# Stick-breaking columns in another order: earlier chains, wider stage spacing, and one pair's T1 built by DMA

## The chip, the cores and the metric

The kernel runs on one core of one Trainium2 chip. The metric is the device time of one execution in microseconds (us). Runs of the kernel before took 2211.62, 2213.59 and 2213.69 us, a median of 2213.59 us.

The engines are named as in the profile: PE is TensorE (PEld its weight loads), DVE is VectorE, ACT is ScalarE, POOL is GpSimd, SP is SyncE.

## The reference, cut to what matters

One layer of an encoder over 256 tokens of width 2048, all in float32: a SwiGLU feed-forward network (FFN), a mixer, a second FFN and an output gate, with layer norms between them. The mixer projects the normalised activations by one wide matrix `w_in` and feeds two attention branches:

```python
proj = x @ w_in
mq, mk, mv, mo, mi, mf, sq, sk, sv, ga, gb = _split_cols(proj)
y_m  = ...  # mLSTM, 4 heads of 256, from mq, mk, mv, gates mi and mf; times sigmoid(mo)
y_sb = _stick_breaking(_heads(sq, 8), _heads(sk, 8), _heads(sv, 8))   # 8 heads of 128
merged = sigmoid(ga) * (y_m @ w_up_m) + sigmoid(gb) * (y_sb @ w_up_sb)
return merged @ w_out
```

Stick-breaking attention, for each head and strictly causal (s < t):

```python
z = q @ k.T * dh ** -0.5
log_one_minus = where(strict, log_sigmoid(-z), 0)
cum = cumsum(log_one_minus); rem = cum[..., -1:] - cum
att = where(strict, exp(log_sigmoid(z) + rem), 0)
out = att @ v
```

## The kernel before, in words

**Matmuls.** Every weight matrix is cut into tiles of 256 rows by up to 512 columns (a *raw*, 512 KB), loaded by SP (`loads`, L1115). ACT casts a raw to a high part (L1142) and DVE subtracts to get the low part (L1146); the two are a *split*. A *unit* is one weight tile for one half of the tokens: six matmuls (L1191 to L1193) into one PSUM bank. A *group* is one block of up to 512 output columns: eight weight tiles for the 2048 rows, two units each, two banks.

**The order of work** is written out by hand as the list `program`. It is walked unit by unit; each unit adds 1.2966 to a planner's clock `sched.now`. Side work is a generator that yields delays (`DELAY`) and is resumed by `sched.run` after the unit at which it is due, so it enters each engine's queue at that point and the engines take their queues in order. Splits are made up to six tiles ahead and a limited number of raws is held (`HELD`: seven and six in the mode "wide", five and six in "mix").

**Pairs.** `seven` computes a pair of column blocks for both halves of the tokens with seven block products in place of eight (a Strassen scheme). Products 1 and 2 come first; then, in each of four quarters of the rows, products 5, 7, 6, 4 and 3, whose five accumulators stay open over all quarters. The weight combinations T1 = B11 + B12 and so on are made in place on the raws: by DVE (`plus`, L345), or, with `loaded`, T1 (and T3 of the last quarter) by an accumulating POOL DMA onto a loaded raw (L1119). The FFN uses `loaded`; the mixer's pairs, made by `both7`, do not. Products 5, 7, 6 and 3 use sums of the activations' quarters: `forms_later` (L309) adds high and low parts, and `form_turn` (L292 to L302) makes the combinations.

**The mixer's order** (L918 to L999): q and k columns of the mLSTM, with the gate columns and stick columns 0 and 1 in the second group (`gates_done`); v; o; then stick columns in groups of four heads, in plain order: 2 to 5, 6 to 9, 10 to 13, 14 to 17 (columns 0 to 7 are q heads, 8 to 15 k heads, 16 to 23 v heads). Then `weave` interleaves a main list (start of the sticks, stick columns 18 to 21 and 22 and 23, the gate branches of block 0, and three rounds of `ups`) with pairs 1, 2 and 3: three pair units after every four main units.

**Stick columns.** `sb_columns` evacuates a group's accumulator by ACT: v heads straight to their place (L684), q and k heads to a temporary (L688), which `sb_turn` transposes on PE 4.6 later (L694) and copies on DVE (L700), two heads a copy.

**Sticks.** `sticks` (L936) starts two chains: heads 0, 2, 4, 6, and 12.0 later heads 1, 3, 5, 7. A stick (L877) waits for its q, k and v, then: scores on PE (L882); ACT's scale, absolute value, exponential and logarithm, all at L225; DVE's maximum and sum (L891) and causal mask (L814); PE's running sum by a triangular matrix (L895, L896); DVE's subtraction (L897); ACT's exponential; DVE's mask (L814); PE's product with v (L906); and the evacuation by ACT (L269) and DVE (L270). Between the steps lie the delays sa, s0, s1, s2, s3, s4. `in_sequence` starts the next stick of a chain with no delay. Each PE result takes one of eight PSUM banks, which the groups and pairs use too. The sticks' results are read by the second half of `ups(0)`.

**mLSTM heads** (L816) run as two chains of two; DVE's product at L832 is followed, m1 later, by PE's L842.

Of the kernel before, what the change touches and what calls it, by code (L numbers as in the profile page):

```python
# [44 lines left out]
DELAY = {  # L45
    "alpha": 24.0, "away": 5.0, "sig": 1.5, "form": 18.0, "ln_turn": 3.6, "ln_step": 2.1, "gb": 14.0, "h": 8.0, "silu": 6.0, "late": 9.0, "rest": 1.2, "mt": 3.2,
    "sbt": 4.6, "g0": 3.0, "g1": 4.0, "g2": 12.0, "cv0": 1.0, "cv1": 3.5, "cv2": 1.3,
    "m0": 3.0, "m1": 0.6, "m2": 0.6, "m3": 4.6, "m4": 4.6, "sa": 1.4, "s0": 6.0, "s1": 6.0, "s2": 3.0, "s3": 4.0, "s4": 4.0,
}


# [113 lines left out]
def flat(pairs):  # L165
    return [u for p in pairs for u in p]
# [7 lines left out]
def kernel(  # L174
# [33 lines left out]
    def big(shape=(P, 1024)):  # L208
        return page_pool.tile(list(shape), F32, name="big", tag="page")
# [102 lines left out]


    def rows_of(w, r, col0, cols):
        return Raw(w[r:r + 2 * P, col0:col0 + cols].rearrange("(k p) c -> p k c", p=P), cols)

    def plain(raw):
        return Weight(raw, [raw], [raw])
# [11 lines left out]
    def seven(wa, ca, wb, cb, rows, cols, act, done, loaded):  # L330

        n = rows // (4 * P)
        accs = {m: {} for m in range(1, 8)}

        def unit(m, i, tile, src, half, sub):  # L340
            return Unit(tile, half, accs[m], src, i, sub, i == 0, i == n - 1, lambda ps, t, m=m: done(m, ps))

        def plus(out, a, b):
            def make():
                nc.vector.tensor_tensor(out=out.tile[:, :, :cols], in0=a.tile[:, :, :cols], in1=b.tile[:, :, :cols],  # L345
                                        op=ALU.add)
            return make

        units = []
        for m, sub in ((1, 0), (2, 2)):  # L350
            for i in range(n):
                units.append(unit(m, i, plain(rows_of(wa, (4 * i + sub) * P, ca, cols)), act, 0, sub))
        for i in range(n):
            b11, b12, b22, b21 = (rows_of(w, (4 * i + sub) * P, c, cols)
                                  for w, c, sub in ((wa, ca, 0), (wb, cb, 0), (wb, cb, 2), (wa, ca, 2)))
            if loaded:
                t1 = Raw(b12.src, cols, b11.src)
                first = Weight(t1, [t1], [])
            else:
                t1 = b11  # L360
                first = Weight(t1, [b11, b12], [], plus(b11, b11, b12))
            if loaded and i == n - 1:
                third = Weight(t3 := Raw(b12.src, cols, b22.src), [t3, b22], [t3])
            else:
                third = Weight(b12, [b12, b22] if loaded else [b22], [b12], plus(b12, b12, b22))
            units += [
                unit(5, i, first, act.forms, 0, 0),
                unit(7, i, third, act.forms, 1, 0),
                unit(6, i, Weight(t1, [], [], plus(t1, t1, b22), first), act.forms, 0, 2),
                unit(4, i, Weight(b21, [b21], [t1, b21], plus(b21, t1, b21)), act, 1, 2),  # L370
                unit(3, i, Weight(b22, [], [b22]), act.forms, 1, 2),
            ]
        return units

    def both7(w, ca, cb, act, dest, ready):

        r, held = {}, {}

        def put(k, t, a, b, op):
            nc.vector.tensor_tensor(out=r[k, t], in0=a, in1=b, op=op)  # L380

        def rest():
            u = r[0, 1]
            put(0, 1, held[7], u, ALU.add)
            z = r[1, 1] = dest(1, 1)
            nc.vector.scalar_tensor_tensor(out=z, in0=u, scalar=-1.0, in1=held[5],
                                           op0=ALU.mult, op1=ALU.subtract)
            ready(1, 1)
            return
            yield  # L390

        def done(m, ps):
            held[m] = ps
            if m == 1:
                r[0, 1] = dest(0, 1)
                nc.scalar.copy(r[0, 1], ps)
            elif m == 2:
                r[0, 0] = dest(0, 0)
                put(0, 0, ps, r[0, 1], ALU.add)
                ready(0, 0)  # L400
            elif m == 6:
                r[1, 0] = dest(1, 0)
                put(0, 1, ps, r[0, 1], ALU.add)
                put(1, 0, held[5], r[0, 1], ALU.add)
                sched.spawn(rest(), DELAY["rest"])
            elif m == 4:
                sched.until(lambda: (1, 1) in r)
                put(0, 1, ps, r[0, 1], ALU.add)
                ready(0, 1)
            elif m == 3:  # L410
                put(1, 0, ps, r[1, 0], ALU.subtract)
                ready(1, 0)

        return seven(w, ca, w, cb, D, COL, act, done, False)

    program = []

# [251 lines left out]

    sq0 = 2 * DM * HM + 2 * DM * HM + 2 * HM  # L670

    def sb_columns(ps, t, first, count):

        for which in range(3):
            lo, hi = max(first, 8 * which), min(first + count, 8 * which + 8)
            if lo >= hi:
                continue
            name = ("sq", "sk", "sv")[which]
            src = ps[:, (lo - first) * DS:(hi - first) * DS]
            if which == 2:  # L680
                if (name, t) not in st:
                    st[name, t] = big()
                cs = slice((lo - 16) * DS, (hi - 16) * DS)
                nc.scalar.copy(st[name, t][:, cs], src)  # L684
                flags.update((name, t, h - 16) for h in range(lo, hi))
            else:
                stage = temp()
                nc.scalar.copy(stage[:, :(hi - lo) * DS], src)  # L688
                sched.spawn(sb_turn(name, t, stage, lo - 8 * which, hi - lo), DELAY["sbt"])

    def sb_turn(name, t, stage, h0, n):
        ps = misc([P, 4, P])
        for k in range(n):
            nc.tensor.transpose(ps[:, k], stage[:, k * P:(k + 1) * P], ident[:])  # L694
        a = h0
        while a < h0 + n:
            b = min(h0 + n, (a // 4 + 1) * 4)
            if (name, "T", a // 4) not in st:
                st[name, "T", a // 4] = big().rearrange("q (h s) -> q h s", s=S)
            nc.vector.tensor_copy(out=st[name, "T", a // 4][:, a % 4:a % 4 + b - a, t * P:(t + 1) * P],  # L700
                                  in_=ps[:, a - h0:b - h0])
            a = b
        drop()
        flags.update((name, t, h) for h in range(h0, h0 + n))
        return
        yield

# [3 lines left out]
    def gates_done(ps, t):  # L711
        stage_g[t] = small.tile([P, 2 * HM], F32, name="gst", tag="gst", bufs=2)
        nc.scalar.copy(stage_g[t][:], ps[:, 0:2 * HM])
        sb_columns(ps[:, 2 * HM:], t, 0, 2)
        if t == TT - 1:
            sched.spawn(gates(), DELAY["g0"])

# [196 lines left out]
    def in_sequence(gens):  # L914
        for g in gens:
            yield from g
# [8 lines left out]
        program.extend(flat(group(w_in, range(0, D, 2 * P), 2048 + g * COL, COL, x1T, v_done(g))))  # L925
    for g in range(2):
        program.extend(flat(group(w_in, range(0, D, 2 * P), 3072 + g * COL, COL, x1T, mo_done(g))))
    def sb(first, n):
        return flat(group(w_in, range(0, D, 2 * P), sq0 + first * DS, n * DS, x1T,
                          lambda ps, t: sb_columns(ps, t, first, n)))  # L930

    program.extend(sb(2, 4) + sb(6, 4))
    program.append(lambda: [sched.spawn(forms_later(x1T, c), 14.0 + 14.0 * c) for c in range(4)])
    program.extend(sb(10, 4))

    def sticks():  # L936
        for a in (0, 1):
            sched.spawn(in_sequence([stick(a), stick(a + 2), stick(a + 4), stick(a + 6)]), 12.0 * a)


    mergedT = ActT(act_tile)
# [49 lines left out]
        return lambda k, t: sched.spawn(sigmoid(k, t), DELAY["sig"])  # L991

    def pair(g):
        return both7(w_in, ga0 + g * COL, ga0 + D + g * COL, x1T, gate_dest(g), gate_ready(g))

    program.extend(sb(14, 4))
    main = [sticks] + sb(18, 4) + sb(22, 2) + branch(0, 0) + branch(0, 1) + ups(0) + ups(1) + ups(2)
    mode("wide")
    program.extend(weave(main, pair(1) + pair(2) + pair(3)))  # L999
    mode("mix")  # L1000
# [108 lines left out]
    def loads(most=len(raws)):  # L1109
        while pos["load"] < most and pos["raw"] < (4 if pos["at"] < 6 else limits(pos["split"])[0]):  # L1110
            j = pos["load"]
            r = raws[j]
            r.tile = page_pool.tile([P, 2, COL], F32, name="raw", tag="page")
            for ks in pieces(j):
                nc.sync.dma_start(out=r.tile[:, ks, :r.cols], in_=r.src[:, ks])  # L1115
                if j == 0 and ks.start == 0:
                    load_x(0, 1)
            if r.plus is not None:
                nc.gpsimd.dma_start(out=r.tile[:, :, :r.cols], in_=r.plus, accum_op=ALU.add)  # L1119
            pos["load"] += 1  # L1120
            pos["raw"] += 1

# [106 lines left out]
```

## Time and profile before

| | |
|---|---|
| runs of the kernel before | 2211.62, 2213.59, 2213.69 us |
| the profiled execution | 2210.92 us |
| its span, first to last instruction | 2209.2 us |
| PE busy | 2186.7 us, 99% |
| DVE, ACT, POOL busy | 1873.8, 1294.3, 100.1 us |
| granted TensorE clock, mean | 0.999 |

The profile is of one execution. The page lists each engine's busy time; windows give it for a stretch; the waits say which instruction ended an engine's idle time; the timeline lists instructions with their start in us from the span's start. A row of a timeline ends with the idle time before it and what ended it, in brackets. In the waits the three numbers are the total in us, how often, and the longest. The mixer lies between about 660 and 1340 us.

### The profile page before, as it was taken

The numbers are of one execution on the slowest core, as the hardware profiler recorded it, in microseconds if no ns is written. First come the engines' busy times: TensorE is split into PE (matmuls) and PEld (weight loads), VectorE is DVE, ScalarE is ACT, GpSimd is POOL, SyncE is SP. The second block draws the span as 40 slices with busy tenths as digits, with TensorE's granted clock in tenths as the row PEclk, the third lists the DMA queues.
The fourth block names the chain that finished last, engine by engine and source line by source line (L and its number), as shares of the span: only waits on it lengthen the run. The fifth ranks groups of instructions, "written<-read, shape, count | busy, mean of one in ns | idle before, by whom it ended". The sixth has DMA issues, their size and how long they took to land. (4 is left out here: it accounts for less than half of the span.)

```text
span 2209.2 us, 28143 instructions
## 1 busy us (share of the span) xinstructions
PE 2186.7 (99%) x9990; PEld 1805.3 (82%) x9990; DVE 1873.8 (85%) x2089; ACT 1294.3 (59%) x1566; POOL 100.1 (5%) x88
## 2 busy tenths in 40 slices
PE   9999999999999999999899999999999999999999
PEld 7888888878888888788778888888888887888888
DVE  6999999998987874668879986699999999989774
ACT  7556655565655565545686554655565565656372
POOL 0100010000010000000000000000010001000000
PEclk9999999999999999999999999999999999999999
DMA  9899999999993675565768886589999999999553
GB/s 334 252 307 298 284 283 313 303 303 270 319 326 106 219 242 158 165 189 157 215 185 249 271 282 212 183 238 294 308 265 306 324 290 294 286 304 338 202 162 105
DMA packets 292365, 560.12 MB, mean 254 GB/s; under 512 B 17624, under 2 KB 26752, under 8 KB 292224
## 3 DMA queue, kind: packets, MB, share of 16 engines
q1 hardware_dynamic: 270464, 516.38, 70.0%
q0 software_dynamic: 21760, 41.95, 11.1%
q8 instruction: 78, 1.28, 0.2%
q14 instruction: 63, 0.52, 0.1%
HBM read 554.06 MB, written 4.19 MB: 253 GB/s over the span
## 5 line engine op out<-in xcount | busy, mean ns | idle before, releaser
L1146 DVE TENSOR_TENSOR split<-raw,split 128x1024 fp32r<-128x1024 f32 (+2 forms) x1049 | 1221.9, 1202 | 165.8 <-ACT split L1142 157.2
L1142 ACT CAST split<-raw 128x1024 fp32r<-128x1024 f32 (+2 forms) x1049 | 1043.2, 1036 | 503.6 <-DVE raw L345 184.8
L1191 PE MATMUL mm<-split,actT 128*128 128x512 f32 (+2 forms) x3128 | 1220.1, 390 | 6.4 <-DVE actT L270 3.1
L1192 PE MATMUL mm<-split,actT 128*128 128x512 f32 (+2 forms) x3128 | 1206.5, 386 | 1.7 <-DVE split L1146 1.5
L1193 PE MATMUL mm<-split,actT 128*128 128x512 f32 (+2 forms) x3128 | 1206.7, 386 | 0.6 <-DVE actT L282 0.6
L1191 PEld LDWEIGHTS mm<-split,actT 128*128 128x128 f32 x3128 | 588.7, 188 | 123.5 <-issue 3.8
L1192 PEld LDWEIGHTS mm<-split,actT 128*128 128x128 f32 x3128 | 588.8, 188 | 120.4 <-DVE split L1146 7.6
L1193 PEld LDWEIGHTS mm<-split,actT 128*128 128x128 f32 x3128 | 588.1, 188 | 121.0 <-DVE actT L282 1.4
L345 DVE TENSOR_TENSOR raw<-raw 128x1024 f32<-128x1024 f32 x224 | 273.3, 1220 | 2.3
L1119 POOL DMA_DIRECT2D raw<-in_ffn_w_dram x80 | 95.5, 1193 | 1879.4 <-DVE temp L543 812.3
L277 ACT CAST actT<-ms 128x512 fp32r<-128x512 f32 x60 | 35.0, 584 | 86.8 <-PE ms L275 85.8
L552 DVE TENSOR_TENSOR temp<-mm,temp 128x512 f32<-128x512 f32 x112 | 76.9, 686 | 5.6 <-PE mm L1193 3.8
L605 DVE SCALAR_TENSOR_TENSOR big<-mm,big 128x512 f32<-128x512 f32 x96 | 65.4, 685 | 16.3 <-PE mm L1193 16.1
L282 DVE TENSOR_TENSOR actT<-ms,actT 128x512 fp32r<-128x512 f32 x60 | 40.8, 684 | 22.9 <-ACT actT L277 11.7
L221 ACT ACT_TABLE_LOAD x35 | 44.9, 1283 | 0.6
L270 DVE TENSOR_TENSOR actT<-temp,actT 128x512 fp32r<-128x512 f32 x40 | 26.5, 688 | 17.3 <-ACT actT L269 17.2
L225 ACT ACTIVATE temp<-mm 128x512 f32<-128x512 f32 (+1 forms) x22 | 12.3, 560 | 44.1 <-PE mm L1193 44.1
L269 ACT CAST actT<-temp 128x512 fp32r<-128x512 f32 x40 | 24.2, 621 | 17.0 <-DVE temp L293 15.2
L225 ACT ACTIVATE temp<-temp 128x512 f32<-128x512 f32 (+1 forms) x48 | 28.5, 594 | 2.5 <-DVE temp L552 1.6
L780 DVE SCALAR_TENSOR_TENSOR temp<-ms,cw,temp 128x253 f32<-128x253 f32 (+2 forms) x48 | 23.1, 481 | 7.3 <-ACT temp L225 6.2
L225 ACT ACTIVATE rstd<-mv,eps 128x1 f32<-128x1 f32 x6 | 1.8, 295 | 45.9 <-DVE mv L462 45.9
L1012 DVE SCALAR_TENSOR_TENSOR big<-big,mm 128x512 f32<-128x512 f32 x8 | 5.5, 686 | 26.9 <-PE mm L1193 26.9
(126 smaller groups left out, 563.3 us busy)
## 6 DMA issues: line engine op xcount, KB each, us to landing
raw<-in_ffn_w_dram SPq DMA_DIRECT2D x655, 512.0 KB, 6.4
raw<-in_w_in_dram SPq DMA_DIRECT2D x192, 512.0 KB, 4.3
raw<-in_ffn_w_dram POOLq DMA_DIRECT2D x80, 512.0 KB, 9.1
raw<-in_w_out_dram SPq DMA_DIRECT2D x32, 512.0 KB, 5.1
raw<-in_w_ple_gate_dram SPq DMA_DIRECT2D x24, 512.0 KB, 5.7
raw<-in_w_up_m_dram SPq DMA_DIRECT2D x16, 512.0 KB, 5.4
raw<-in_w_up_sb_dram SPq DMA_DIRECT2D x16, 512.0 KB, 5.7
raw<-in_w_ple_gate_dram SPq DMA_DIRECT2D x16, 256.0 KB, 4.7
```

Of the source, the lines that this page charges most:

```text
L221: nc.scalar.preload_act_table_set(table[0])
L225: nc.scalar.activation(out, in_, func, **kw)
L282: nc.vector.tensor_tensor(out=dst[:, 1], in0=ps[:], in1=dst[:, 0], op=ALU.subtract)
L345: nc.vector.tensor_tensor(out=out.tile[:, :, :cols], in0=a.tile[:, :, :cols], in1=b.tile[:, :, :cols], op=ALU.add)
L552: nc.vector.tensor_tensor(out=out, in0=a, in1=b, op=op)
L605: nc.vector.scalar_tensor_tensor(out=xs, in0=ps, scalar=0.5, in1=xs, op0=ALU.mult, op1=ALU.add)
L1119: nc.gpsimd.dma_start(out=r.tile[:, :, :r.cols], in_=r.plus, accum_op=ALU.add)
L1142: nc.scalar.copy(hi[:, ks], r[:, ks])
L1146: nc.vector.tensor_tensor(out=lo[:, ks], in0=r[:, ks], in1=hi[:, ks], op=ALU.subtract)
L1191: nc.tensor.matmul(ps, hi, w[0][:, k, :u.cols], start=first, stop=False)
L1192: nc.tensor.matmul(ps, hi, w[1][:, k, :u.cols], start=False, stop=False)
L1193: nc.tensor.matmul(ps, lo, w[0][:, k, :u.cols], start=False, stop=last)
```

## The change

- **Order of the columns.** After the mLSTM's o columns come v heads 0 to 3, then a group of k heads 0, 1 and q heads 2, 3. Then the sticks start, ahead of the next groups (k 2, 3 and q 4, 5; v 4 to 7). The weave's main list begins with k 4, 5 and q 6, 7, then k 6, 7. The number and width of the groups are as before. A group of four q and k heads has two column ranges, so each of its raws is loaded by two DMAs of 256 columns.
- **Turns.** The copies after the transposes go from DVE to ACT, two heads a copy.
- **Sums of quarters.** `forms_later` starts after the first stick group, at 6, 24, 42 and 60, where it started after the second, at 14, 28, 42 and 56.
- **Stages.** m0, m1, m2 from 3.0, 0.6, 0.6 to 4.0, 2.0, 1.4; s0, s1, s3, s4 from 6.0, 6.0, 4.0, 4.0 to 7.0, 7.6, 5.0, 6.0; the second chain starts 14.0 after the first, not 12.0.
- **T1 of pair 1.** `both7` passes on `loaded`, true for pair 1 alone.

```diff
-    "m0": 3.0, "m1": 0.6, "m2": 0.6, "m3": 4.6, "m4": 4.6, "sa": 1.4, "s0": 6.0, "s1": 6.0, "s2": 3.0, "s3": 4.0, "s4": 4.0,
+    "m0": 4.0, "m1": 2.0, "m2": 1.4, "m3": 4.6, "m4": 4.6, "sa": 1.4, "s0": 7.0, "s1": 7.6, "s2": 3.0, "s3": 5.0, "s4": 6.0,
...
     def rows_of(w, r, col0, cols):
-        return Raw(w[r:r + 2 * P, col0:col0 + cols].rearrange("(k p) c -> p k c", p=P), cols)
+        ranges = col0 if isinstance(col0, list) else [(col0, cols)]
+        return Raw([w[r:r + 2 * P, c:c + n].rearrange("(k p) c -> p k c", p=P) for c, n in ranges], cols)
...
-        return seven(w, ca, w, cb, D, COL, act, done, False)
+        return seven(w, ca, w, cb, D, COL, act, done, loaded)
...
+    def sb_turn(t, stage, heads):
         ps = misc([P, 4, P])
-        for k in range(n):
+        for k in range(len(heads)):
             nc.tensor.transpose(ps[:, k], stage[:, k * P:(k + 1) * P], ident[:])
...
-            nc.vector.tensor_copy(out=st[name, "T", a // 4][:, a % 4:a % 4 + b - a, t * P:(t + 1) * P],
-                                  in_=ps[:, a - h0:b - h0])
...
+            nc.scalar.copy(st[name, "T", h // 4][:, h % 4:h % 4 + 2, t * P:(t + 1) * P], ps[:, k:k + 2])
...
-    program.extend(sb(2, 4) + sb(6, 4))
-    program.append(lambda: [sched.spawn(forms_later(x1T, c), 14.0 + 14.0 * c) for c in range(4)])
-    program.extend(sb(10, 4))
+    program.extend(sb(16, 17, 18, 19))
+    program.append(lambda: [sched.spawn(forms_later(x1T, c), 6.0 + 18.0 * c) for c in range(4)])
+    program.extend(sb(8, 9, 2, 3))
...
-            sched.spawn(in_sequence([stick(a), stick(a + 2), stick(a + 4), stick(a + 6)]), 12.0 * a)
+            sched.spawn(in_sequence([stick(a), stick(a + 2), stick(a + 4), stick(a + 6)]), 14.0 * a)
...
-        return both7(w_in, ga0 + g * COL, ga0 + D + g * COL, x1T, gate_dest(g), gate_ready(g))
+        return both7(w_in, ga0 + g * COL, ga0 + D + g * COL, x1T, gate_dest(g), gate_ready(g), g == 1)
...
-    program.extend(sb(14, 4))
-    main = [sticks] + sb(18, 4) + sb(22, 2) + branch(0, 0) + branch(0, 1) + ups(0) + ups(1) + ups(2)
+    program.append(sticks)
+    program.extend(sb(10, 11, 4, 5) + sb(20, 21, 22, 23))
+    main = sb(12, 13, 6, 7) + sb(14, 15) + branch(0, 0) + branch(0, 1) + ups(0) + ups(1) + ups(2)
...
-                nc.sync.dma_start(out=r.tile[:, ks, :r.cols], in_=r.src[:, ks])
+                at = 0
+                for src in r.src:
+                    n = src.shape[-1]
+                    nc.sync.dma_start(out=r.tile[:, ks, at:at + n], in_=src[:, ks])
+                    at += n
```

More of the change, by code (lines that the diff above doesn't have):

```diff
@@ L373, in seven, with both7 @@
         return units
-    def both7(w, ca, cb, act, dest, ready):
+    def both7(w, ca, cb, act, dest, ready, loaded):
         r, held = {}, {}
@@ L670 @@
     sq0 = 2 * DM * HM + 2 * DM * HM + 2 * HM
[L672 to L689, printed above, removed]
@@ L691, in sb_turn, with sb_columns @@
-    def sb_turn(name, t, stage, h0, n):
+    def sb_columns(ps, t, heads):
+        n = len(heads) * DS
+        if heads[0] >= 16:
+            if ("sv", t) not in st:
+                st["sv", t] = big()
+            c0 = (heads[0] - 16) * DS
+            nc.scalar.copy(st["sv", t][:, c0:c0 + n], ps[:, :n])
+            flags.update(("sv", t, h - 16) for h in heads)
+        else:
+            stage = temp()
+            nc.scalar.copy(stage[:, :n], ps[:, :n])
+            sched.spawn(sb_turn(t, stage, heads), DELAY["sbt"])
@@ L692, in sb_turn @@
+    def sb_turn(t, stage, heads):
         ps = misc([P, 4, P])
-        for k in range(n):
+        for k in range(len(heads)):
             nc.tensor.transpose(ps[:, k], stage[:, k * P:(k + 1) * P], ident[:])
[L695 to L700, printed above, removed]
-                                  in_=ps[:, a - h0:b - h0])
-            a = b
+        for k in range(0, len(heads), 2):
+            name, h = ("sq", "sk")[heads[k] // 8], heads[k] % 8
+            if (name, "T", h // 4) not in st:
+                st[name, "T", h // 4] = big().rearrange("q (h s) -> q h s", s=S)
+            nc.scalar.copy(st[name, "T", h // 4][:, h % 4:h % 4 + 2, t * P:(t + 1) * P], ps[:, k:k + 2])
+            flags.update([(name, t, h), (name, t, h + 1)])
@@ L703, in sb_turn @@
         drop()
-        flags.update((name, t, h) for h in range(h0, h0 + n))
         return
@@ L713, in gates_done @@
         nc.scalar.copy(stage_g[t][:], ps[:, 0:2 * HM])
-        sb_columns(ps[:, 2 * HM:], t, 0, 2)
+        sb_columns(ps[:, 2 * HM:], t, (0, 1))
         if t == TT - 1:
@@ L927, with sb @@
         program.extend(flat(group(w_in, range(0, D, 2 * P), 3072 + g * COL, COL, x1T, mo_done(g))))
-    def sb(first, n):
-        return flat(group(w_in, range(0, D, 2 * P), sq0 + first * DS, n * DS, x1T,
-                          lambda ps, t: sb_columns(ps, t, first, n)))
-    program.extend(sb(2, 4) + sb(6, 4))
-    program.append(lambda: [sched.spawn(forms_later(x1T, c), 14.0 + 14.0 * c) for c in range(4)])
-    program.extend(sb(10, 4))
+    def sb(*heads):
+        if heads[0] >= 16:
+            col0 = sq0 + heads[0] * DS
+        else:
+            col0 = [(sq0 + h * DS, 2 * DS) for h in heads[::2]]
+        return flat(group(w_in, range(0, D, 2 * P), col0, len(heads) * DS, x1T,
+                          lambda ps, t: sb_columns(ps, t, heads)))
+    program.extend(sb(16, 17, 18, 19))
+    program.append(lambda: [sched.spawn(forms_later(x1T, c), 6.0 + 18.0 * c) for c in range(4)])
+    program.extend(sb(8, 9, 2, 3))
     def sticks():
         for a in (0, 1):
-            sched.spawn(in_sequence([stick(a), stick(a + 2), stick(a + 4), stick(a + 6)]), 12.0 * a)
+            sched.spawn(in_sequence([stick(a), stick(a + 2), stick(a + 4), stick(a + 6)]), 14.0 * a)
     mergedT = ActT(act_tile)
@@ L1118, in loads @@
             if r.plus is not None:
-                nc.gpsimd.dma_start(out=r.tile[:, :, :r.cols], in_=r.plus, accum_op=ALU.add)
+                nc.gpsimd.dma_start(out=r.tile[:, :, :r.cols], in_=r.plus[0], accum_op=ALU.add)
             pos["load"] += 1
```

## The prediction

> **What bounds the kernel now.** The page comes first: its span and the busy shares.
>
> ```profile
> span 2209.2 us, 28143 instructions
> PE 2186.7 (99%) x9990; PEld 1805.3 (82%) x9990; DVE 1873.8 (85%) x2089; ACT 1294.3 (59%) x1566; POOL 100.1 (5%) x88
> ```
>
> TensorE (PE) is idle for only 22.5 us (2209.2 - 2186.7). The change removes no matmul, so it can win little more than PE's stops in the mixer. The table of 20 us windows over 880 to 1200 us shows where these lie; the columns are PE, PEld, DVE, ACT and POOL busy, the granted clock, the DMA share and GB/s.
>
> ```profile
> 880.00:900.00 20.00, 19.11 (x88) 15.30 (x87) 8.64 (x16) 9.75 (x15) 0.00 (x0) 1.00 0.54 157
> ...
> 920.00:940.00 20.00, 18.23 (x83) 14.96 (x83) 12.36 (x24) 11.18 (x16) 0.00 (x0) 1.00 0.58 172
> ...
> 980.00:1000.00 20.00, 20.00 (x94) 16.55 (x93) 14.14 (x21) 11.17 (x14) 0.00 (x0) 1.00 0.59 184
> ...
> 1020.00:1040.00 20.00, 20.00 (x91) 16.35 (x90) 19.69 (x27) 14.36 (x20) 0.00 (x0) 1.00 0.53 146
> 1040.00:1060.00 20.00, 16.96 (x84) 13.77 (x83) 18.36 (x25) 14.02 (x23) 0.00 (x0) 1.00 0.59 169
> 1060.00:1080.00 20.00, 19.97 (x110) 17.83 (x111) 17.70 (x21) 12.61 (x17) 0.00 (x0) 0.91 0.71 215
> 1080.00:1100.00 20.00, 17.31 (x87) 14.41 (x86) 17.40 (x21) 12.24 (x18) 0.00 (x0) 1.00 0.79 247
> ...
> 1140.00:1160.00 20.00, 17.18 (x74) 13.12 (x73) 16.36 (x19) 14.97 (x21) 0.00 (x0) 1.00 0.61 175
> ...
> sum 320.00, PE 307.72 PEld 252.42 DVE 241.33 ACT 196.35 POOL 0.00; mean PE 19.23 PEld 15.78 DVE 15.08 ACT 12.27 POOL 0.00
> ```
>
> Idle PE: 320 - 307.72 = **12.28 us**. Of it 2.66 lie in 880 to 940 (0.89 + 1.77, the mLSTM heads), 5.76 in 1040 to 1100 (3.04 + 0.03 + 2.69) and 2.82 in 1140 to 1160, both among the stick-breaking chains. The clock of 0.91 in one window costs 20 x 0.09 = **1.8 us** more. PE's waits in the mixer say for whom.
>
> ```profile
> PE mm L1191 <- DVE actT L270: 3.1, 2, 2.7
> PE ms L842 <- DVE temp L832: 2.7, 2, 1.8
> PE ms L895 <- DVE temp L814: 2.1, 2, 1.9
> PE ms L882 <- DVE actT L270: 2.1, 1, 2.1
> PE mm L1191 <- ACT big L684: 1.0, 1, 1.0
> PE mm L1192 <- DVE split L1146: 0.8, 1, 0.8
> ```
>
> Almost all are waits for VectorE (DVE). The timeline shows the dearest: first PE's rows, then DVE's.
>
> ```profile
> 1088.57 0.85 PE L906 MATMUL ms<-temp,big 128*128 128x256 f32 x4
> 1089.26 0.82 PE L882 MATMUL ms<-big 128*128 128x256 f32 x4
> 1092.76 0.47 PE L1191 MATMUL mm<-split,actT 128*128 128x512 f32 x1 [2.69 <-DVE actT L270]
> ```
>
> ```profile
> 1088.30 3.49 DVE L1146 TENSOR_TENSOR split<-raw,split 128x1024 fp32r<-128x1024 f32 x3
> 1091.71 0.28 DVE L270 TENSOR_TENSOR actT<-ms,actT 128x128 fp32r<-128x128 f32 x1
> 1092.32 0.29 DVE L270 TENSOR_TENSOR actT<-ms,actT 128x128 fp32r<-128x128 f32 x1 [0.33 <-ACT actT L269]
> ```
>
> A stick's last product (L906) and the next stick's first (L882) each take a PSUM bank. A woven pair holds five accumulators and the main group two, of eight banks, so a hand-over has one left. The bank comes free when DVE has evacuated it at L270, and L270 stands behind three splits. I call this a hand-over in the tight phase (pair 1 past its first eight units, about 1040 to 1100). A stop also costs more than its idle time, since matmuls overlap:
>
> ```profile
> 923.20 0.40 PE L1193 MATMUL mm<-split,actT 128*128 128x512 f32 x1
> 925.36 0.67 PE L842 MATMUL ms<-big,temp 128*128 128x257 f32 x2 [1.77 <-DVE temp L832]
> ```
>
> Start to start is 2.16 us where rows 0.23 apart are usual: 1.93 lost for 1.77 idle, 0.16 more. Over some ten stops that is 1.6. In all 12.28 + 1.8 + 1.6 = **15.7 us** are there to win: 3.0 in the mLSTM and 12.7 in the sticks.
>
> **The change part by part.** *mLSTM spacing.* The schedule steps once per unit, six matmuls or 1.36 us. One unit now covers L832 before L842; m1 of 2.0 makes it two. The stop of 0.90 goes, the one of 1.77 shrinks to 0.4: of 3.0 us I leave 0.5, **gain 2.5**. The heads end some 8 us later, hidden: by the program's order their results are read two branch groups after the sticks' columns, past 1150.
>
> *Order of columns and start of the sticks.* Group ends show in ScalarE's (ACT's) evacuations; the sticks' ends in L882 and L906.
>
> ```profile
> 961.00 0.65 ACT L688 COPY temp<-mm 128x256 f32<-128x256 f32 x2 [0.71 <-PE mm L1193]
> ```
>
> ```profile
> L882 PE MATMUL ms<-big x32: 272/377/589, 1007.6 to 1137.8; 128*128 128x256 f32 x16, 128*128 128x128 f32 x16
> L906 PE MATMUL ms<-temp,big x32: 272/326/454, 1042.7 to 1176.0; 128*128 128x256 f32 x16, 128*128 128x128 f32 x16
> ```
>
> Now the first stick runs from 1007.6 to 1042.7, 35 us for 24.4 of scheduled delays, and the last ends at 1176. After, the second group ends at 961 and its turn takes 5, so the first L882 comes at about 966. The delays sum to 30.0, so a stick takes 41. Sticks 0 and 2 fill 966 to 1048, sticks 1 and 3 run 15 us later to 1063. Sticks 4 and 5 need keys 4 and 5, now in the first woven group. The weave begins two groups of 16 x 1.36 = 22 us after 961, at 1005; its first group lies among 28 units (16 + 12 woven), 38 us, and with 5 for stops and the sticks' own matmuls it ends at 1048, its turn at 1053. So the chains run 1053-1094-1135 and 1063-1104-1145, and end 30 us sooner, before pair 2's five products fill the banks. Two sticks lie wholly ahead of the tight phase, and DVE has 14.14 of 20 busy there. Hand-overs 0-2 and 1-3 move out of it; 2-4 is broken by the wait for keys; 3-5 (1063) stays in and 4-6 (1094) at its edge. So of the 8.1 us at 1040 to 1100 (5.76 idle, 1.8 clock, three stops x 0.16) one and a half stops of 2.85 (2.69 + 0.16) stay, 4.3: **gain 3.8**.
>
> *Stages further apart.* s1 and s4 grow by one or two units, 1.4 to 2.7 us, against L814 waits of at most 1.9: 2.1 + 0.4 idle + 0.5 overlap, **gain 3.0**. The split wait (0.8 + 0.2) and a last stop of 0.37 near 1180 stand beside late sticks; with their overlap 1.6, **gain 1.5**.
>
> *Sums of quarters sooner.* Eight adds at L309 and what follows them:
>
> ```profile
> L309 DVE TENSOR_TENSOR big<-actT x8: 681/684/687, 972.3 to 1027.6; 128x512 f32<-128x512 f32 x8
> ```
>
> The last moves from 1027, where DVE has 19.69 of 20, to about 1001. Same work; counted in the 3.8. Uncovered, it would delay unit 5 of a quarter; it comes sooner, so nothing is late.
>
> *Turn copies to ACT.* Sixteen DVE copies (L700) become ACT copies, and three groups load by two DMAs a tile, 24 more SP issues.
>
> ```profile
> L700 DVE COPY big<-ms x16: 402/417/426, 751.7 to 1014.9; 128x256 f32<-128x256 f32 x16
> ```
>
> DVE loses 16 x 0.417 = 6.7 us; ACT, 11.17 of 20 busy there, gains 16 x 0.33 (half of the pair of 0.65) = 5.2. Both hidden under PE's matmuls: 0, and without that cover 5 either way. I put 0.3 for new stops of the early chain.
>
> *T1 of pair 1 by loads.* Four T1 adds and the last quarter's T3 add go from DVE; five accumulating POOL DMAs of 512 KB come, 2.6 MB, where the DMA share is 0.59 to 0.79.
>
> ```profile
> L345 DVE TENSOR_TENSOR raw<-raw 128x1024 f32<-128x1024 f32 x224 | 273.3, 1220 | 2.3
> ```
>
> ```profile
> L1119 POOL DMA_DIRECT2D raw<-in_ffn_w_dram x80: 1176/1189/1318, 56.6 to 2009.7; - x80
> ...
>   ACT split L1142: 95.4, 40
> ...
> DMA to landing us min/median/max: 5.8/9.1/12.5
> ```
>
> ```profile
> 120.00:160.00 40.00, 40.00 (x182) 33.12 (x181) 37.50 (x41) 23.10 (x26) 2.37 (x2) 1.00 0.94 289
> ```
>
> DVE loses 5 x 1.22 = 6.1 us in the tight phase. The new wait is ACT's: its cast of T1 waits for SP's load, then POOL's add (9.1 median), and behind it queue the sticks' exponentials and the PSUM copies, for which PE waits. In the FFN 40 of 80 such casts waited, 2.4 us each, while PE stayed at 40.00 of 40 in the FFN's window above. Bounds: a gain of 6.1, if all DVE relief reaches PE; a loss of 5 x 5.5 = 27.5 (ACT's longest wait, next part), if every wait does. I take a loss of 0.5, by the FFN's row.
>
> **Sum:** 2.5 + 3.8 + 3.0 + 1.5 - 0.3 - 0.5 = **10.0 us**. The profiled execution took 2210.92 (span 2209.2 and 1.7 around it), 2.7 under the median of 2213.59, to which I apply the gain: **2203.6 us**.
>
> [...] After a stop of 2.09 us, 256-wide matmuls stand 0.22 apart; before it, 0.12:
>
> ```profile
> 1049.76 0.28 PE L1193 MATMUL mm<-split,actT 128*128 128x256 f32 x1
> 1049.88 0.28 PE L1191 MATMUL mm<-split,actT 128*128 128x256 f32 x1
> ...
> 1061.35 0.41 PE L1192 MATMUL mm<-split,actT 128*128 128x256 f32 x1
> 1061.57 0.41 PE L1193 MATMUL mm<-split,actT 128*128 128x256 f32 x1
> ```
>
> [...] The 80 issues took 1176 to 1318 ns beside a DVE at 37.50 of 40, so five would stretch by 0.6 at most.
>
> **The rivals.**
>
> ```profile
> ACT split L1142 <- DMA raw<-in_ffn_w_dram: 48.6, 18, 5.5
> ```
>
> *A, all stops go* (the free banks and DVE's relief do more than I grant): 15.7, so 2197.9. For it: two sticks leave the tight phase. Against: 3-5 stays in.
> *B, the stops come back*: keys 4 to 7 now come latest, so four of eight sticks still run in the weave, 10 us apart instead of 15, and collide. Then only mLSTM and spacing win, less one more stop: 2.5 + 3.0 - 0.8 - 2.85 = 1.9, so 2211.7. In this case the change does what it says for the first four sticks alone.
> *C, late T1, slower*: seven raws are held, up to three by an open quarter, so T1 is asked for four raws ahead, some 9 us at 2.2 us each (a quarter's 5 units and 6.7 main ones, 11.7 x 1.36 = 16 us, use 7.3 raws), against 9.1 for the add alone. If each of five casts holds ACT for the 5.5 us of the row above and PE waits along, it is 27.5 - 10.5 = 17 slower, 2231. It decides from 10.5 / 5 = 2.1 us per cast that reach PE. Against: six split weights stand ahead of PE.
>
> **How the numbers follow.** Forecast 0.48 (2199 to 2208), A 0.20, B 0.18, C 0.14. About 0.2% (4.4 us) is what a measurement of this kernel can tell from no change. Faster is forecast and A, 0.68; same is B, 0.18; slower is C, 0.14. The range reaches from under A (2196) past B to 2214 and leaves out C and the edge of A.
>
> **What would show it.** First L882 near 966 and last L906 near 1145; no stop at L842 over 0.5; no PE wait for L814; idle PE in 880 to 1200 near 5; five POOL issues near 1030 to 1090. I am wrong if ACT's casts wait there for w_in DMAs while PE stops, or if L882 or L1191 still waits for L270 three times or more.

## The result: 7 us slower, with one new stop of 12 us

The changed kernel takes 2220.48 us (median of 7 runs, 2216.17 to 2222.62), the kernel before 2213.59 (7 runs, 2211.62 to 2215.18): a ratio of 1.0032, 95% interval 1.0020 to 1.0043. The forecast was 2203.6, faster.

Line numbers have moved. In the changed kernel a stick's scores are L875 (L882 before), its maximum and sum L884 (L891), its mask L807 (L814), its running sum L888 and L889 (L895, L896), DVE's subtraction L890 (L897), its product with v L899 (L906). The splits are L1144 (ACT) and L1148 (DVE), the DVE sums L346, the accumulating POOL DMA L1121, the turn L690 and its copy L695, and the mLSTM's L825 and L835 are L832 and L842 of before. Kernels that hold stick 5 back have two lines more from the stick on: there the running sum is L890.

The first lines of the changed kernel's page:

```profile
span 2220.0 us, 28172 instructions
PE 2190.5 (99%) x9990; PEld 1809.1 (81%) x9990; DVE 1864.9 (84%) x2068; ACT 1294.7 (58%) x1574; POOL 106.1 (5%) x93
```

The span grew by 10.8 us (this execution took 2221.73, above the median). DVE has less to do, as intended. The table of 20 us windows over 880 to 1200 us, with the columns as in the prediction:

```profile
920.00:940.00 20.00, 17.90 (x75) 14.47 (x74) 11.47 (x22) 10.49 (x17) 0.00 (x0) 0.91 0.45 132
...
1040.00:1060.00 20.00, 19.97 (x103) 16.82 (x101) 15.64 (x21) 12.98 (x21) 1.19 (x1) 1.00 0.66 186
1060.00:1080.00 20.00, 18.33 (x102) 16.45 (x103) 13.62 (x17) 12.52 (x20) 1.20 (x1) 0.91 0.67 188
1080.00:1100.00 20.00, 8.09 (x38) 6.50 (x37) 9.83 (x11) 4.94 (x5) 1.19 (x1) 0.67 0.70 223
...
1160.00:1180.00 20.00, 16.08 (x64) 12.80 (x63) 15.98 (x17) 9.01 (x13) 0.00 (x0) 0.91 0.60 195
...
sum 320.00, PE 300.36 PEld 248.34 DVE 226.75 ACT 190.67 POOL 5.95; mean PE 18.77 PEld 15.52 DVE 14.17 ACT 11.92 POOL 0.37
```

Idle PE went from 12.28 to 320 - 300.36 = 19.64 us. The stops of before at 1040 to 1060 and 1140 to 1160 are gone, as forecast; but one window, 1080 to 1100, has 11.91 us of idle PE, and around 1060 and 1160 there are new ones. PE's waits in the mixer name them:

```profile
PE ms L888 <- DVE temp L890: 11.9, 1, 11.9
PE mm L1193 <- DVE actT L270: 3.9, 1, 3.9
PE ms L835 <- DVE temp L825: 2.1, 1, 2.1
PE ms L875 <- ACT temp L225: 1.0, 1, 1.0
PE ms L875 <- ACT big L695: 0.7, 1, 0.7
```

No wait for the mask (L814 before) is left, as the wider stages promised. The 11.9 us are a single stop. Its timeline, engine by engine: PE, DVE, ACT, POOL.

```profile
1083.83 0.81 PE L888 MATMUL ms<-temp,tri 128*128 128x384 f32 x2
1084.47 0.39 PE L889 MATMUL ms<-temp,ones 128*128 128x128 f32 x2
1096.77 1.65 PE L888 MATMUL ms<-temp,tri 128*128 128x384 f32 x2 [11.91 <-DVE temp L890]
```

```profile
1092.76 1.23 DVE L1148 TENSOR_TENSOR split<-raw,split 128x1024 fp32r<-128x1024 f32 x1 [6.49 <-ACT split L1144]
1093.90 1.22 DVE L346 TENSOR_TENSOR raw<-raw 128x1024 f32<-128x1024 f32 x1
1095.04 1.22 DVE L1148 TENSOR_TENSOR split<-raw,split 128x1024 fp32r<-128x1024 f32 x1
1096.17 0.55 DVE L890 TENSOR_TENSOR temp<-temp,ms 128x384 f32<-128x384 f32 x1
```

```profile
1091.68 1.99 ACT L1144 CAST split<-raw 128x1024 fp32r<-128x1024 f32 x2 [8.12 <-DMA raw<-in_w_in_dram]
```

```profile
1082.40 1.19 POOL L1121 DMA_DIRECT2D raw<-in_w_in_dram  x1 [7.42 <-DMA raw<-in_w_in_dram]
```

It reads backwards. PE's second L888 belongs to the other chain's stick. It needs a PSUM bank, and the only one is held by the first stick's running sum until DVE has subtracted it (L890). L890 stands in DVE's queue behind three full-size instructions; the first of them waits for ACT's cast, and that for a loaded tile. The tile is T3 of pair 1's last quarter: POOL could start its add only at 1082.40, after 7.42 us of waiting for SP's load; the add landed 9.2 us after that, and ACT's cast began at 1091.68.

Two sticks are at the same step at the same time because both had waited for the same keys:

```profile
967.89 0.81 PE L875 MATMUL ms<-big 128*128 128x256 f32 x4
976.74 0.81 PE L875 MATMUL ms<-big 128*128 128x256 f32 x4
...
1056.62 0.82 PE L899 MATMUL ms<-temp,big 128*128 128x256 f32 x4
...
1059.37 0.60 PE L690 MATMUL ms<-ident,temp 128*128 128x128 f32 x4
1060.71 0.92 PE L875 MATMUL ms<-big 128*128 128x256 f32 x4 [0.73 <-ACT big L695]
1062.59 0.76 PE L875 MATMUL ms<-big 128*128 128x256 f32 x2 [0.96 <-ACT temp L225]
```

Sticks 0 and 1 start at 967.9 and 976.7, and stick 3 ends with its L899 at 1057. The turn of keys 4 and 5 (L690) ends at 1060, and sticks 4 and 5 start at 1060.7 and 1062.6 (a stick's scores are four matmuls, merged in one row for the first of the two; the second stick's wait for ACT to free a bank). In step they stay: sticks 4 and 5 end and 6 and 7 begin within 1.3 us of each other, at 1116.5 to 1118.5, and both end together again at 1156. From 1160.5 the next group's L1193 waits 3.9 us for a bank behind L270.

So the **theory**: two sticks in step, with one free bank, make the stop, and a late T3 lengthens it. **Rivals**: the late T3 alone; the sticks in step alone; the T1 loads in general; the wider stages; ACT's turn copies.

### The profile page after: what moved, and what is told of

Same layout as the page of the kernel before. It is cut to its first block, busy times and chain, and to the rows that moved or that the text cites. A ratio compares the mean times of both kernels' runs of the same rounds, so it can differ in the third digit from the quotient of the medians.

```text
span 2220.0 us, 28172 instructions
## 1 busy us (share of the span) xinstructions
PE 2190.5 (99%) x9990; PEld 1809.1 (81%) x9990; DVE 1864.9 (84%) x2068; ACT 1294.7 (58%) x1574; POOL 106.1 (5%) x93
## 4 chain that ended last, share of the span: by engine, by line
PE 91%; DMA 3%; DVE 3%; issue 2%; ACT 0%; SPq 0%; DVEq 0%; POOLq 0%; ACTq 0%
PE mm L1194 29%; PE mm L1193 29%; PE mm L1195 29%; DMA raw<-in_ffn_w_dram 2%; DVE split L1148 2%; PE ms L275 1%; DMA raw<-in_w_in_dram 1%; DVE raw L346 1%; PE ms L480 0%; ACT split L1144 0%; PE ms L875 0%; PE ms L835 0%; PE ms L888 0%; DVE actT L282 0%; DVE big L606 0%
## 5 line engine op out<-in xcount | busy, mean ns | idle before, releaser
L1148 DVE TENSOR_TENSOR split<-raw,split 128x1024 fp32r<-128x1024 f32 (+2 forms) x1049 | 1223.1, 1200 | 184.1 <-ACT split L1144 169.5
L1144 ACT CAST split<-raw 128x1024 fp32r<-128x1024 f32 (+2 forms) x1049 | 1045.1, 1036 | 519.6 <-DVE raw L346 165.3
L1193 PE MATMUL mm<-split,actT 128*128 128x512 f32 (+2 forms) x3128 | 1221.2, 390 | 5.4 <-DVE actT L270 3.9
L1193 PEld LDWEIGHTS mm<-split,actT 128*128 128x128 f32 x3128 | 589.7, 189 | 122.4 <-issue 5.0
L346 DVE TENSOR_TENSOR raw<-raw 128x1024 f32<-128x1024 f32 x219 | 266.9, 1219 | 2.1
L1121 POOL DMA_DIRECT2D raw<-in_ffn_w_dram x80 | 95.5, 1193 | 1452.3 <-DMA raw<-in_ffn_w_dram 403.3
L270 DVE TENSOR_TENSOR actT<-temp,actT 128x512 fp32r<-128x512 f32 x40 | 26.5, 687 | 17.7 <-ACT actT L269 17.6
```

The costliest lines, as they stand in the source:

```text
L1121: nc.gpsimd.dma_start(out=r.tile[:, :, :r.cols], in_=r.plus[0], accum_op=ALU.add)
L1144: nc.scalar.copy(hi[:, ks], r[:, ks])
L1148: nc.vector.tensor_tensor(out=lo[:, ks], in0=r[:, ks], in1=hi[:, ks], op=ALU.subtract)
L1193: nc.tensor.matmul(ps, hi, w[0][:, k, :u.cols], start=first, stop=False)
```

## The experiments

Times are medians; each ratio, with its 95% interval, is to the kernel before, which was run again on the same chip beside each group of kernels. Its medians were 2211.6 to 2213.6, so a difference between two times of the table can carry some 2 us that the ratios do not.

| kernel | us | ratio |
|---|---|---|
| changed | 2220.5 | 1.0032 [1.0020, 1.0043] |
| changed, T3 by DVE | 2215.0 | 1.0013 [1.0004, 1.0022] |
| changed, no loads | 2214.8 | 1.0011 [1.0002, 1.0021] |
| before, with the loads | 2211.1 | 1.0002 [0.9992, 1.0012] |
| changed, stick 5 held 12.0 | 2204.5 | 0.9970 [0.9957, 0.9983] |
| both: stick 5 held, T3 by DVE ("mended") | 2200.1 | 0.9947 [0.9933, 0.9960] |
| changed, turn copies on DVE | 2220.2 | 1.0035 [1.0023, 1.0047] |
| before, new m0 to m2 | 2212.4 | 1.0005 [0.9996, 1.0014] |
| changed, old delays | 2209.1 | 0.9988 [0.9979, 0.9997] |
| mended, m1 4.6 | 2197.1 | 0.9929 [0.9917, 0.9942] |
| mended, old s0, s1, s3, s4 | 2203.4 | 0.9959 [0.9946, 0.9973] |
| stick 5 held, no loads | 2197.1 | 0.9932 [0.9920, 0.9945] |
| T3 by DVE, old delays, late start | 2215.6 | 1.0020 [1.0011, 1.0029] |
| stick 5 held, no loads, m1 4.6 | **2192.9** | 0.9918 [0.9904, 0.9932] |
| the same, turn copies on DVE | 2201.8 | 0.9954 [0.9942, 0.9967] |

**T3 by DVE, T1 still by loads.**

```diff
-            if loaded and i == n - 1:
+            if loaded is True and i == n - 1:
...
-        return both7(..., gate_ready(g), g == 1)
+        return both7(..., gate_ready(g), "t1" if g == 1 else False)
```

> The changed kernel, but T3 of pair 1's last quarter is made by DVE again; its four T1 stay accumulated by POOL (four POOL issues, not five). Theory (the 12 us stop of PE at 1084.6 comes from ACT's wait of 8.1 us for that T3): the stop goes, 10 to 14 us less than the changed kernel, 2207 to 2211. Rival 1 (the two sticks in step with one free bank make the stop by themselves): within 3 us of 2220. Rival 2 (late T1 loads cost as well): half goes, 2213 to 2216.

2215.0, 5.5 us less (4.2 by the ratios): the half, not the whole. PE's wait for L890 shrank to 7.1 us and did not go:

```profile
PE ms L888 <- DVE temp L890: 7.1, 1, 7.1
```

**No loads at all.**

```diff
-        return both7(..., gate_ready(g), g == 1)
+        return both7(..., gate_ready(g), False)
```

> The changed kernel with all of pair 1's sums on DVE as before (no POOL issue in the mixer), so the new order, spacing, turns and early sums alone. Theory (late T3): the stop goes, and DVE's 6.1 us more in the tight phase cost 0 to 3: 2207 to 2213. Rival 1 (sticks in step): within 3 us of 2220 or slower. If the T1 loads help as the change supposes, it is 2 to 4 us slower than the kernel with T3 alone on DVE.

2214.8, above what the theory of the late T3 gave, and much as long as with the four T1 by loads (2215.0), so these are not what is left. Its DVE timeline shows what is left of the stop when no load is late:

```profile
1080.66 1.23 DVE L346 TENSOR_TENSOR raw<-raw 128x1024 f32<-128x1024 f32 x1
1081.81 2.35 DVE L1148 TENSOR_TENSOR split<-raw,split 128x1024 fp32r<-128x1024 f32 x2
1084.08 1.22 DVE L346 TENSOR_TENSOR raw<-raw 128x1024 f32<-128x1024 f32 x1
1085.21 1.22 DVE L1148 TENSOR_TENSOR split<-raw,split 128x1024 fp32r<-128x1024 f32 x1
1086.35 0.55 DVE L890 TENSOR_TENSOR temp<-temp,ms 128x384 f32<-128x384 f32 x1
```

```profile
1080.88 0.38 PE L889 MATMUL ms<-temp,ones 128*128 128x128 f32 x2
1086.95 1.65 PE L888 MATMUL ms<-temp,tri 128*128 128x384 f32 x2 [5.69 <-DVE temp L890]
```

Five instructions of 1.22 us stand ahead of L890, queued before PE got to the first stick's sum, and PE waits for all of them. With these delays, sticks in step stop PE for 5.7 us without any load.

**The loads alone, in the kernel before** (`both7` takes `loaded` and passes it on, true for pair 1).

> The kernel before with T1 and the last T3 of pair 1 made by loads, nothing else. If the late T3 alone makes the stop: 8 to 12 us slower than before, 2221 to 2226. If it needs the two sticks in step (theory): ACT waits about 8 us there too, but PE stops for less than 5 of it: 2211 to 2218.

2211.1, no difference that can be measured, though ACT waited for such a DMA for 7.2 us there (two waits; the one for T3 was 5.0, not 8.1). There sticks 2 and 3 start 9.6 us apart, and no second stick wants the bank during that wait; idle PE in 880 to 1200 is 12.30 us, as in the kernel before (12.28). So a late T3 need not stop PE. The next kernel shows that it can, by another way.

**Stick 5 held back**, so that the chains leave step.

```diff
         yield from wait(*[(n, t, h) for n in ("sq", "sk", "sv") for t in range(TT)])
+        if h == 5:
+            yield 12.0
```

> The changed kernel with a delay of 12.0 ahead of head 5's stick, so that sticks 4 and 5, and 6 and 7 after them, run 12 apart and no longer in step. Theory (T3 late and sticks in step together make the stop): ACT still waits about 8 us for T3, PE's stop shrinks below 5 us and the one of 4 us at 1160 goes: 2208 to 2213. If the late T3 alone stops PE: 2217 to 2222.

2204.5, 16 us less than the changed kernel (14 by the ratios) and 7 less than before, more than expected. The waits for L890 and L270 are gone; the late T3 shows by itself. PE's waits, then ACT's row:

```profile
PE mm L1195 <- ACT temp L684: 5.3, 1, 5.3
PE ms L835 <- DVE temp L825: 2.1, 1, 2.1
PE ms L877 <- ACT big L695: 0.7, 1, 0.7
```

```profile
1084.57 2.94 ACT L1146 CAST split<-raw 128x1024 fp32r<-128x1024 f32 x3 [5.08 <-DMA raw<-in_w_in_dram]
1087.42 0.36 ACT L684 COPY temp<-mm 128x256 f32<-128x256 f32 x1
```

ACT's evacuation of a finished group (L684) stands behind the cast that waits for T3, and a new group waits for the bank.

**Both edits.**

> The changed kernel with stick 5 held 12.0 later and T3 of pair 1's last quarter made by DVE (both edits of the two earlier runs). In the run with stick 5 later a stop of 5.3 us was left, PE waiting for ACT's evacuation at L684 while ACT waited 5.1 us for the loaded T3. Theory (late T3 and sticks in step are two causes that add): the 5.3 us go as well, 4 to 6 us under the 2204.5 of that run, 2198 to 2201. Rival (with the sticks apart that wait only moves a stop that DVE or ACT would make anyway): 2203 to 2206.

2200.1, 4.4 us less again. Idle PE in 880 to 1200 was 19.64 us in the changed kernel, 14.81 with T3 alone by DVE and 8.10 with stick 5 alone held; with both it is 3.10 (320 - 316.90). So the two causes add:

```profile
sum 320.00, PE 316.90 PEld 261.93 DVE 246.24 ACT 206.11 POOL 4.77; mean PE 19.81 PEld 16.37 DVE 15.39 ACT 12.88 POOL 0.30
```

**Turn copies back on DVE, in the changed kernel** (`nc.vector.tensor_copy` for `nc.scalar.copy` in `sb_turn`).

> The changed kernel with the copies after the turns back on DVE. If ACT's copies make the two stops of 0.9 and 1.1 us at 1060 (PE's L875 waits for ACT's L695 and L225) and the slow clock behind them: 2 to 4 us less than the changed kernel, 2216 to 2219. If the key turn is simply the last thing that both chains wait for, whoever copies: within 1.5 us of 2220.5.

2220.2: no difference. The stops at 1060 stay, and the one behind L695 only changes its engine (DVE, 0.9 us; ACT's was 0.7). Whoever copies, the key turn is the last thing that both chains wait for.

**The mLSTM's delays alone, in the kernel before.**

> The kernel before with m0, m1, m2 of 4.0, 2.0, 1.4 and nothing else. The prediction's term: 2.5 us faster than before. From the changed kernel's trace, where one stop went and the other stayed at 2.1 us with a slow clock behind it: no more than 1 us from before.

2212.4 beside 2212.2 for before: nothing. One of two stops went, the other grew from 1.77 to 2.1 us. Idle PE in 880 to 1200 fell by 0.85 us (12.28 to 11.43), but the granted clock of 920 to 940 fell from 1.00 to 0.91.

**All delays as before, in the changed kernel.**

> The changed kernel with all delays of before (m0 to m2, s0 to s4, second chain 12.0 after the first): order, early start, ACT turns, early sums and loads alone. The sticks 4 and 5 still wait for the same keys and run in step, so the stop at L888 stays at 6 to 12 us: 2216 to 2222. If wider stages were worth the 3.0 us of the prediction it is 3 slower than the changed kernel, 2222 to 2225; if the wider stages themselves make the stop, 2208 to 2213.

2209.1: 11 us under the changed kernel (10 by the ratios) and a little under before (0.9988). The theory's 2216 to 2222 was missed: sticks 4 and 5 start in step here too, at 1060.0 and 1061.9. The wider stages and the offset of 14.0, in this place, lose, and being in step does not by itself make a stop of 12 us. Its PE waits 3.4 us for L890 where the changed kernel waited 11.9. ACT's timeline shows that the late T3 is nearly as late, 7.18 us; DVE's, that stick 4's L890 came first:

```profile
1088.17 1.99 ACT L1144 CAST split<-raw 128x1024 fp32r<-128x1024 f32 x2 [7.18 <-DMA raw<-in_w_in_dram]
```

```profile
1085.08 0.55 DVE L890 TENSOR_TENSOR temp<-temp,ms 128x384 f32<-128x384 f32 x1
```

With the old delays L890 ran 3 us before that cast was released; with the new ones it stood behind it. A shift of a few us in the hand-written schedule decided whether PE felt the late tile.

**m1 of 4.6, in the mended kernel.**

> The mended kernel (stick 5 held 12.0 later, T3 by DVE; 2200.1) with m1 of 4.6 in place of 2.0. Two more units stand between L825 and L835 in the mLSTM. Theory (the stop of 2.1 us at 924 is DVE's backlog of some 2 us ahead of L825): it goes, 1.5 to 2.5 less, 2197.5 to 2198.7. Rival (the backlog moves along with it): within 1 of 2200.

2197.1, 3.0 us less: the stop at L835 goes altogether, and idle PE in 880 to 1200 falls from 3.10 to 1.05 us. The term was there; m1 of 2.0 was too small to win it, since DVE's backlog up to L825 is longer than one unit: in the changed kernel a split, the mask and L825 end 2.23 us after the split's start (924.36 to 926.59), and a unit takes 1.36.

**Old s0, s1, s3, s4, in the mended kernel.**

> The mended kernel with s0, s1, s3, s4 as before (6.0, 6.0, 4.0, 4.0). If wider stages are worth the prediction's 3.0 us: PE waits for L807 again, 2202 to 2204. If the early start and the sticks apart already cover those waits: within 1.5 of 2200.

2203.4, 3.3 us slower (2.7 by the ratios, whose intervals overlap). Idle PE in 880 to 1200 rises from 3.10 to 6.73 us (320 - 313.27), with the waits for the mask back:

```profile
PE ms L901 <- DVE temp L807: 2.3, 2, 1.6
PE ms L835 <- DVE temp L825: 2.1, 1, 2.1
PE ms L890 <- DVE big L381: 1.5, 1, 1.5
```

(L901 is the product with v, L890 here the running sum.) So with the sticks apart wider stages are worth about what was forecast.

**No loads, sticks apart.**

> The mended kernel with no loads in pair 1 at all: its sums on DVE, stick 5 held 12.0 later. If the T1 loads relieve PE by way of DVE's 4 x 1.22 us: 2 to 5 slower, 2202 to 2205. If that relief stays hidden: within 1.5 of 2200.

2197.1, 3.0 us faster, not slower. DVE has 251.22 us of work in 880 to 1200 instead of 246.24, and PE's idle time is the same (2.9 instead of 3.1).

**Late start**, with T3 by DVE and the old delays (`sticks` back at the head of the weave).

> The changed kernel with T3 by DVE, all delays as before, and the start of the sticks moved back into the weave, so no chain begins sooner (and with no hold on stick 5: the keys are there when each stick comes). If the early start is what wins: stops as before in 1040 to 1190, 2208 to 2213. If order, early sums and T1 loads win without it: 2200 to 2205.

2215.6, slower than both forecasts. The chains of before come back (sticks 0 to 3 start at 1006, 1020, 1041 and 1059; before, at 1008, 1021, 1049 and 1060), and with them stops like theirs. The profiled execution took 2221.2, 5.7 above the median:

```profile
PE ms L875 <- DVE actT L270: 5.3, 2, 3.0
PE ms L899 <- DVE temp L890: 4.6, 2, 2.6
PE ms L835 <- DVE temp L825: 2.7, 2, 1.8
PE ms L888 <- DVE temp L807: 2.5, 2, 1.9
```

The kernel with the old delays and the early start took 2209.1 even with the late T3, 6.5 us less. The two differ in T3 as well, but T3 by DVE made the kernel faster, not slower, wherever it was tried. So the early start wins; order, early sums and T1 loads without it do not.

**No loads, m1 of 4.6, sticks apart**, and then the same with turn copies on DVE.

> The mended kernel with m1 of 4.6 and no loads in pair 1 at all. If T1 by loads costs some 3 us even with the sticks apart: 2193 to 2195. If it costs nothing and the difference of the two earlier runs was chance: 2196 to 2198. If it helps: 2199 or more.

> The run just named, with the copies after the turns back on DVE. By the prediction's 0 for this part: within 1.5 us of it. If ACT's copies relieve DVE where it counts: 2 to 4 slower. If they make the stop of 0.9 us at 1056: 0.5 to 1.5 faster.

2192.9 for the first, the fastest of all: 0.9918 of before. Idle PE in 880 to 1200 is down to 0.78 us (320 - 319.22), with a single wait of 0.7 left:

```profile
sum 320.00, PE 319.22 PEld 264.41 DVE 254.08 ACT 209.53 POOL 0.00; mean PE 19.95 PEld 16.53 DVE 15.88 ACT 13.10 POOL 0.00
```

It is 4.2 us under the run with T1 by loads, as the pair before was 3.0 under (2.4 and 3.3 by the ratios). With the sticks in step the two kinds were alike (2214.8 and 2215.0). The intervals of each pair overlap and the traces of the first two pairs show only 0.2 to 0.3 us of idle PE between them, so what is shown is that T1 by loads wins nothing here; whether it costs 2 to 4 us with the sticks apart stays open.

With the copies on DVE it took 2201.8, 8.9 more. Here a turn waits for DVE:

```profile
1089.01 0.44 PE L690 MATMUL ms<-ident,temp 128*128 128x128 f32 x2 [2.16 <-DVE big L695]
```

```profile
1087.40 1.22 DVE L1150 TENSOR_TENSOR split<-raw,split 128x1024 fp32r<-128x1024 f32 x1
1088.54 0.42 DVE L695 COPY big<-ms 128x256 f32<-128x256 f32 x1
```

The copy of 0.42 us that frees the turn's bank stands behind full-size splits. Idle PE in 880 to 1200 rises by 2.8 us (316.45 instead of 319.22), and the granted clock of 1080 to 1100 falls from 1.00 to 0.91, some 1.8 us more. The two profiled spans differ by 6.7; 1.7 of that is idle PE outside these windows, and the rest was not placed.

## Why the prediction was wrong

- **The step that failed** is the timing of the chains: "So the chains run 1053-1094-1135 and 1063-1104-1145". The text saw that sticks 4 and 5 both need the first woven group's keys, put its turn at 1053 and let stick 3 end at 1063, which kept them 10 us apart. In the trace stick 3 ended near 1057 and the turn at 1060, so both were waiting and left together. The delay between the chains, 14.0 on paper, was already only 9 us (first L875 at 967.9 and 976.7), because the first chain had its turn to wait for and the second had not. The gain of 3.8 in 1040 to 1100 was worked out from chains 10 us apart; idle PE there rose instead, from 5.76 to 13.61 us, 11.91 of it in one stop. Holding stick 5 back is worth 16 us (14 by the ratios). The sign that the prediction named came with it: ACT's cast waited for a w_in DMA while PE stopped.
- **Rival B** named the mechanism (late keys, the sticks collide in the tight phase) and mis-sized it: one more stop of 2.85 us. In step, the stop at L888 lasted until DVE had worked through its queue up to L890, which frees the bank: 5.7 us with nothing late, 11.9 with a late tile, and 3.4 with the old delays, where the late tile stood behind L890.
- **Rival C** named the late loads and mis-sized them the other way: five waits of 5.5 us that PE shares. ACT waited for the four T1 4.9 us in all, in two waits; for T3 8.1 us at once. T3 is asked for right behind the last T1 and used right behind it, and its add had to wait 7.42 us for SP's load. It cost about 5 us in both places: 5.5 in the changed kernel and 4.4 with the sticks apart (4.2 and 5.1 by the ratios). The forecast's own term of 0.5 was too small by that.
- **mLSTM spacing, gain 2.5**: 0 measured. One unit more was not enough; three give 3.0, of which the trace shows 2.05 as idle PE.
- **Stages further apart, gain 3.0**: 3.3 measured with the sticks apart, but a loss in step, since there it moved L890 behind the late cast.
- **Start of the sticks, gain 3.8 in 1040 to 1100**: right in kind. The stops of before in 1040 to 1060 and 1140 to 1160 went, and without the early start the kernel with the old delays takes 6.5 us more.
- **Turn copies, 0**: right in the changed kernel (2220.2 and 2220.5), wrong where nothing else stops PE (8.9).
- **T1 by loads through DVE's relief**: no gain in any pair.
- **The ceiling of 15.7 us** for everything was low by 3: with the sticks apart, no loads and m1 of 4.6 the kernel is 18.9 us under the kernel before that was run beside it (2211.79). The two profiled spans differ by 17.5 (2209.2 and 2191.7). Idle PE makes 13.6 of it: 12.28 - 0.78 = 11.5 in 880 to 1200, and 2.1 outside, which the prediction left aside. PE's busy time makes the other 3.9, for which it had 1.8 of slow clock and 1.6 of overlap.
- **Not taken out by themselves** were the two DMAs per tile of the new groups and the earlier sums of quarters. The fastest kernel has both.

## What to carry to other kernels

The two chains of sticks began 8.9 us apart (967.9 and 976.7), waited for the same keys and left them 1.9 us apart (1060.7 and 1062.6). Where chains of side work wait for the same event, look for that event before counting on an offset, and add the offset behind it. When accumulators fill all PSUM banks but one, price a hand-over by what stands in the evacuating engine's queue, not by the evacuation: here L890 takes 0.55 us, and PE stopped for 3.4 to 11.9. T3 passed two DMAs one after the other: its add waited 7.42 us for SP's load and landed 9.2 us after its start. It may have to be asked for sooner; no kernel here did so.

## What the runs showed of the hardware

In the changed kernel a stop of 2.10 us at 924 came with a granted clock of 0.91 for 920 to 940; before, stops of 1.77 at 924 and 2.69 at 1090 left it at 1.00, and one of 2.09 at 1058 came with 0.91 for 1060 to 1080. The stop ahead of L835 (L842 before) is 2.07 to 2.12 us long in nine of the kernels: the clock of 920 to 940 was 0.91 in five of them (the changed kernel among them) and 1.00 in four (the mended one among them). By the same 20 x 0.09 as in the prediction, an estimate, that can put some 1.8 us between two kernels whose stop there is the same. The rows after the stop at 924 show the slower pace, 512-wide matmuls 0.43 us apart instead of 0.23:

```profile
926.74 1.20 PE L835 MATMUL ms<-big,temp 128*128 128x257 f32 x2 [2.10 <-DVE temp L825]
927.37 0.99 PE L1193 MATMUL mm<-split,actT 128*128 128x512 f32 x1
928.15 0.63 PE L1194 MATMUL mm<-split,actT 128*128 128x512 f32 x1
928.58 0.63 PE L1195 MATMUL mm<-split,actT 128*128 128x512 f32 x1
```

Stops of 2.07 to 2.12 us came out both ways, so in these runs the length alone did not decide the clock; what else did, no run here shows.

The changed kernel's five POOL adds of the mixer were issued in 1185 to 1198 ns each, beside a DVE busy for 4.83 of those 5.97 us (in the FFN, 80 in 1176 to 1318), and took 5.6 to 9.8 us to land.
